# Down projection with seven products per pair of tiles, five pairs at a time

## The chip, the core and the metric

The kernel runs on one core of a Trainium2 chip. The core has a matrix engine (TensorE, PE; it writes only to the PSUM banks), a vector engine (VectorE, DVE), a scalar engine (ScalarE, ACT), a general engine (GpSimd, POOL) and a queue that starts transfers (SyncE, SP). Each works through its own list of instructions in order, and they meet through semaphores. The metric is the time of one execution on the device in microseconds (us), the median of three runs.

## What is computed

One step of a decoder layer on 536 rows: 16 meta tokens and 512 prompt tokens, and 8 single-token samples; the last part of the layer works on 520 of them (8 + 512), all in fp32. After attention, pooling and the output projection, the part that matters here is

```python
a = jax.nn.silu(jnp.einsum('btd,df->btf', h1, w_gate)) * jnp.einsum('btd,df->btf', h1, w_up)
ff = jnp.einsum('btf,fd->btd', a, w_down)
return layer_norm(DEEPNORM_ALPHA * h1 + ff, ln2_g, ln2_b)
```

with a model width of 2048 (16 tiles of 128) and an inner width of 5632 (44 tiles of 128). The outputs are the new rows and the new caches.

## The kernel before

**Number format.** Every matmul operand is split into a high part, rounded to the PE's one-pass format (fp32r), and the rest: `split` (L177) makes `wh` on ACT (L182) and `wl` on DVE (L183) for a piece of weights, in a ring of five buffers of 512 columns each (`WB`). A product is then three matmuls, high x high, high x low and low x high (`products`, L186, matmuls on L189, L190, L192). Activations lie with the token on the free axis, 520 columns, in two halves of 260 (`HALF`).

**Gate and up.** The 44 inner tiles are taken as 22 pairs, tile i with tile i + 22. For each pair, gate and up (`Set.run`, L962) each compute a 2 x 2 block (two inner tiles by two token halves) with seven products instead of eight, a Winograd form of Strassen's method: sums of the weight quarters are made on DVE (L926), sums of the activations were made once, and the products are accumulated in PSUM and added on DVE and ACT (L972 to L996). A product is 8 x 3 = 24 matmuls, a pair 2 x 7 x 24 = 336. `gate_out` applies SiLU, `up_out` multiplies (L1013, L1014, L1016) and stores the two tiles of `a` to memory (`a_d`, L1015 and L1017). Each pair takes six buffers (two of gate, two of up, one of each `run`) from a ring of 16 rows of 520 columns (`row_tile`).

**Down.** The 44 tiles of `a` are read back in four chunks of 11 (`load_a`, L1050), split, and kept. For every chunk and each of the 16 output tiles `down` (L1061) loads the weights (512 and 192 KB), splits them and runs 11 x 2 x 3 = 66 matmuls; DVE adds the two PSUM halves to `acc[m]` (L1080, L1082). The last chunk runs twice through the output tiles, once for each part of the tokens (264 and 256 columns, `DHALF`), so that its weights are loaded and split twice.

**The end.** After every fourth output tile of the last chunk, `Rows.part` turns four tiles back to tokens on rows (PE transposes, L1109), copies them out (L1111) and takes statistics (L1112). After each part of the tokens `Rows.end` applies the closing LayerNorm on DVE (L1119, L1120, 512 columns each) and stores the result. What the first part leaves runs beside the second part's matmuls.

**Order of the work.** A planner orders the instructions of each engine before the run by estimated times; an instruction that stands earlier in the program has priority where several are ready, and weight loads, weight sums and splits are moved ahead by 400 places (`WPRIO`). On the chip the order is fixed: an engine waits at the head of its queue. The operands of gate and up fill all 56 buffers of 520 columns (`slot`, `NG`); the tiles of `a` later take over these buffers. One memory plan (`Region`, `Pool`) hands parts of the on-chip memory from stage to stage.

Of the kernel before, what the change touches and what calls it, by code (L numbers as in the profile page):

```python
# [22 lines left out]
NTOK = NS + SEQ  # L23
HN = NTOK // 2
# [5 lines left out]
F_TILES = 44  # L30
NPAIR = F_TILES // 2
CH = 11
NCH = F_TILES // CH
ALPHA = 2.0 ** 0.25
# [4 lines left out]
NF = 5  # L39
# [8 lines left out]
NG = 56  # L48
NZ = 19
FRW, RRW, MDW = 18960, 24368, 9880  # L50
WIDTH = {"pts": 512}
# [4 lines left out]
SWAP = [i + 8 if i < 8 else i - 8 if i < 16 else i for i in range(32)]  # L56
HALF = [slice(0, HN), slice(HN, NTOK)]

ASLOTS = [[*range(32, 40), *range(14)], [14, 15, *range(24, 32), *range(16, 24), *range(40, 44)],
          [*range(44, 56), *range(32, 40), 0, 1], [*range(2, 24)]]  # L60
DHALF = [slice(0, NS + 256), slice(NS + 256, NTOK)]


# [1 line left out]
def hybrid_step(ctx, tc, xin, w_in, w_o, w_g, w_u, w_d, w_pool, par_d, cst_d, ident_d, ln2gb, kct_d, vc_d, hist_d,  # L65
                ck_d, cv_d, sp_d, yp, ys, nkp, nvp, npp, nks, nvs, nps):
    nc = tc.nc
    PS = bass.MemoryType.PSUM
    sb = ctx.enter_context(tc.tile_pool(name="sb", bufs=1))
    dp = ctx.enter_context(tc.tile_pool(name="dp", bufs=1, space=bass.MemoryType.DRAM))  # L70
# [70 lines left out]

    h_d = dp.tile([KT, P, NTOK], F32, name="h_d")
    h1_d = dp.tile([KT, P, NTOK], F32, name="h1_d")
    a_d = dp.tile([F_TILES, P, NTOK], F32, name="a_d")

    def row_tile(name, w=NTOK):

        return ap_.tile([P, NTOK], F32, tag="row", name=name, bufs=16)[:, :w]
# [22 lines left out]
    def load_raw(src, name):  # L171
        raw = wp.tile([P, 1024], F32, tag="raw", name=f"raw_{name}", bufs=NRAW)[:, :src.shape[-1]]
        with tc.high_priority(prio[0]):
            nc.sync.dma_start(raw, src)
        return raw

    def split(s, name, lo=None):  # L177

        n = s.shape[-1]
        wh, wl = [sp[0].tile([P, 512], F32R, tag=t, bufs=sp[1])[:, :n] for t in ("wh", "wl")]  # L180
        with tc.high_priority(prio[0]):
            nc.scalar.copy(wh, s)  # L182
            (lo or nc.vector).tensor_sub(wl, s, wh.bitcast(F32))  # L183
        return wh, wl

    def products(out, wh, wl, hi, lo, first, last, onto=False):  # L186

        for j, o in enumerate(out):
            nc.tensor.matmul(o, wh, hi[j], start=first, stop=False, skip_group_check=onto)  # L189
            nc.tensor.matmul(o, wh, lo[j], start=False, stop=False, skip_group_check=onto)  # L190
        for j, o in enumerate(out):
            nc.tensor.matmul(o, wl, hi[j], start=False, stop=last, skip_group_check=onto)  # L192
# [48 lines left out]
    with ExitStack() as sa:  # L241
        act, pa, px = Pool(rr), Pool(mid, fr, rr), Pool(mid)
        ps = sa.enter_context(tc.tile_pool(name="psA", bufs=4, space=PS))
# [176 lines left out]
        out = kv_banks(0)  # L420
# [370 lines left out]
    ps = ctx.enter_context(tc.tile_pool(name="psB", bufs=8, space=PS))  # L791

    def bank(name, w=HN):
        return ps.tile([P, 512], F32, tag="bank", name=name, bufs=8)[:, :w]
# [214 lines left out]
    def up_out(s, go, i):  # L1009
        uo = [row_tile(f"uo{i}_{j}") for j in range(2)]  # L1010
        (c11, c12), (c21, c22) = [[g[:, x] for x in HALF] for g in uo]
        c = s.run(c11, c12, c21, c22)
        nc.vector.tensor_mul(go[0][:, HALF[0]], go[0][:, HALF[0]], c11)  # L1013
        nc.vector.tensor_mul(go[1], go[1], uo[1])  # L1014
        nc.sync.dma_start(a_d[2 * i + 1], go[1])  # L1015
        nc.vector.tensor_mul(go[0][:, HALF[1]], go[0][:, HALF[1]], c)  # L1016
        nc.sync.dma_start(a_d[2 * i], go[0])  # L1017

    g0 = ln1(0, out_proj(0))
    zs1 = out_proj(1, g0)  # L1020
# [24 lines left out]
        up_out(sets[2 * i + 1], gate_out(sets[2 * i], i), i)  # L1045


    acc = []

    def load_a(c):  # L1050
        hi, lo = [], []
        for f in range(CH):
            t = pb.tile([P, NTOK], F32, tag="fill", name=f"af{c}_{f}", bufs=NF)
            nc.sync.dma_start(t, a_d[c * CH + f])
            hi.append(slot(f"ah{c}_{f}", (NTOK,), ASLOTS[c][2 * f]))
            lo.append(slot(f"al{c}_{f}", (NTOK,), ASLOTS[c][2 * f + 1]))
            nc.scalar.copy(hi[f], t)
            nc.vector.tensor_sub(lo[f], t, hi[f].bitcast(F32))
        return hi, lo

    def down(c, m, a, halves, tag=""):  # L1061
        nm = f"d{c}_{m}{tag}"
        out = [bank(f"{nm}_{j}", s.stop - s.start) for j, s in enumerate(halves)]
        for r, (f0, f1) in enumerate(((0, 8), (8, CH))):
            raw = load_raw(w_d[c, m, :, f0 * P:f1 * P], f"{nm}_{r}")
            for g0 in range(f0, f1, 4):
                ge = min(g0 + 4, f1)
                wh, wl = split(raw[:, (g0 - f0) * P:(ge - f0) * P], f"{nm}_{g0}")
                for f in range(g0, ge):
                    sl = slice((f - g0) * P, (f - g0 + 1) * P)  # L1070
                    products(out, wh[:, sl], wl[:, sl], [a[0][f][:, s] for s in halves], [a[1][f][:, s] for s in halves],
                             f == 0, f == CH - 1)
        if c == 0:
            acc.append(row_tile(f"acc{m}"))
            hb = pb.tile([P, 2, HN], F32, tag="fill", name=f"h1b{m}", bufs=NF).rearrange("p a b -> p (a b)")
            nc.sync.dma_start(hb, h1_d[m])
        for o, s in zip(out, halves):
            t = acc[m][:, s]
            if c == 0:
                nc.vector.scalar_tensor_tensor(t, hb[:, s], ALPHA, o, op0=ALU.mult, op1=ALU.add)  # L1080
            else:
                nc.vector.tensor_add(t, t, o)  # L1082

    a_cur = load_a(0)
    for c in range(NCH - 1):
        for m in range(KT):
            down(c, m, a_cur, HALF)
            if m == 0:
                a_nxt = load_a(c + 1)
        a_cur = a_nxt  # L1090


    pb.close()
    pb, zp = Pool(fr), Pool(Region("mid_c", F32, MDW))
    gb = [[pb.tile([P, 512], F32, name=f"gb{i}_{q}") for q in range(4)] for i in range(2)]
    for i in range(2):
        for q in range(4):
            nc.sync.dma_start(gb[i][q], ln2gb[i:i + 1, q * 512:(q + 1) * 512].to_broadcast([P, 512]))

    class Rows:  # L1100
        def __init__(self, c0, n, dst):
# [22 lines left out]
    for h, rr in ((0, rows[:3]), (1, rows[3:])):  # L1124
        for m in range(KT):
            down(NCH - 1, m, a_cur, [DHALF[h]], f"h{h}")
            if m % 4 == 3:
                for x in rr:
                    x.part(m // 4)
        for x in rr:  # L1130
            x.end()


# [88 lines left out]
```

## Time and profile before

| what | value |
|---|---|
| median of 3 runs | 1990.83 us (1987.53 to 1991.93) |
| the profiled execution: its time, its span | 1997.12 us, 1995.3 us |
| granted PE clock, mean | 0.992 |
| gate and up, seven-product part | about 617 to 1460 us |
| down projection, chunks 0 to 2 | about 1460 to 1840 us |
| last chunk and closing LayerNorm | about 1840 to 1995 us |
| moved by transfers | 277.57 MB |

The profile is of one execution. A line gives engine, source line, operation and tile names, `out<-in`, and durations; "idle before" is the time the engine waited ahead of it, and the name behind the arrow is what ended that wait. A window's row gives the busy time of the five engines in a stretch, then the granted clock, the busy share of the 16 transfer engines and GB/s. Durations of DVE instructions overlap a little where none of them waits: the next starts before the one before has been confirmed.

### The profile page before, as it was taken

How to read it: one execution, taken by the hardware profiler on the slowest of the kernel's cores; microseconds unless marked ns; L12 is line 12 of the kernel's file. 1: busy time of each engine (PE TensorE's matmuls, PEld its weight loads, DVE VectorE, ACT ScalarE, POOL GpSimd, SP SyncE). 2: the span in 40 equal slices, each digit the busy share in tenths (PEclk: the TensorE clock that was granted, in tenths of full speed). 3: DMA queues.
4: the chain of work that ended last, by engine and by line, in shares of the span. 5: the costliest groups of instructions: out<-in, count | busy, mean ns of one | idle time of the engine just before them, and what ended most of it. 6: DMA issues, size and time to landing. Idle time of an engine off the chain costs nothing.

```text
span 1995.3 us, 39815 instructions
## 1 busy us (share of the span) xinstructions
PE 1960.8 (98%) x16051; PEld 1932.7 (97%) x16051; DVE 1336.8 (67%) x2450; ACT 898.1 (45%) x1749; POOL 2.5 (0%) x8
## 2 busy tenths in 40 slices
PE   8999999999999999999999999999999999999996
PEld 8999999999988999999999999999999999999996
DVE  6666657666777888787777777787763533433586
ACT  6644445544654444445554555445542322222442
POOL 0000000000000000000000000000000000000000
PEclk9999999999999999999999999999999999999998
DMA  8732222665754444333333333333374633323554
GB/s 262 226 102 69 65 79 85 198 202 169 243 162 146 143 149 154 127 121 119 118 108 128 113 130 97 129 115 128 114 249 129 197 106 98 113 88 102 165 177 137
DMA packets 106201, 277.57 MB, mean 139 GB/s; under 512 B 12240, under 2 KB 35352, under 8 KB 105912
## 3 DMA queue, kind: packets, MB, share of 16 engines
q1 hardware_dynamic: 104896, 272.93, 42.5%
q8 instruction: 126, 2.06, 0.4%
q10 hardware_dynamic: 1120, 2.10, 0.4%
q14 instruction: 59, 0.48, 0.1%
HBM read 250.11 MB, written 27.41 MB: 139 GB/s over the span
## 4 chain that ended last, share of the span: by engine, by line
PE 94%; DVE 2%; DMA 2%; ACT 1%; issue 0%; SPq 0%; DVEq 0%; ACTq 0%
PE p_u L189 7%; PE p_u L192 7%; PE p_u L190 7%; PE p_g L192 7%; PE p_g L189 7%; PE p_g L190 7%; PE d L192 6%; PE d L190 6%; PE d L189 6%; PE o L189 3%; PE o L192 3%; PE o L190 3%; PE mm_q L189 2%; PE mm_u L189 2%; PE mm_u L192 2%; PE mm_u L190 2%
## 5 line engine op out<-in xcount | busy, mean ns | idle before, releaser
L182 ACT CAST rr<-fr 128x512 fp32r<-128x512 f32 (+1 forms) x1056 | 639.5, 612 | 918.6 <-PE d L190 248.6
L183 DVE TENSOR_TENSOR rr<-fr,rr 128x512 fp32r<-128x512 f32 (+1 forms) x1056 | 698.2, 677 | 411.3 <-ACT rr L182 399.1
L926 DVE TENSOR_TENSOR fr<-fr 128x1024 f32<-128x1024 f32 x176 | 215.3, 1224 | 71.2 <-DMA fr<-in_w_g_dram 39.0
L192 PE MATMUL p_g<-rr 128*128 128x260 f32 x800 | 226.5, 283 | 2.4 <-DVE rr L183 2.4
L189 PE MATMUL p_u<-rr 128*128 128x260 f32 x800 | 226.8, 284 | 1.3 <-DVE fr L991 1.3
L189 PE MATMUL p_g<-rr 128*128 128x260 f32 x800 | 227.2, 284 | 0.5 <-DVE fr L991 0.5
L192 PE MATMUL p_u<-rr 128*128 128x260 f32 x800 | 225.5, 282 | 0.0
L190 PE MATMUL p_g<-rr 128*128 128x260 f32 x768 | 217.3, 283 | 0.0
L190 PE MATMUL p_u<-rr 128*128 128x260 f32 x768 | 216.9, 282 | 0.0
L189 PE MATMUL d<-rr 128*128 128x260 f32 x736 | 191.4, 281 | 0.0
L190 PE MATMUL d<-rr 128*128 128x260 f32 x672 | 175.5, 283 | 0.0
L192 PEld LDWEIGHTS p_g<-rr 128*128 128x128 f32 x800 | 151.6, 189 | 2.7 <-DVE rr L183 2.7
L189 PEld LDWEIGHTS p_u<-rr 128*128 128x128 f32 x800 | 150.6, 188 | 1.8 <-DVE fr L991 1.8
L189 PEld LDWEIGHTS p_g<-rr 128*128 128x128 f32 x800 | 151.1, 189 | 0.8 <-DVE fr L991 0.7
L192 PEld LDWEIGHTS p_u<-rr 128*128 128x128 f32 x800 | 151.1, 189 | 0.0
L192 PE MATMUL d<-rr 128*128 128x260 f32 x736 | 148.2, 282 | 0.0
L189 PE MATMUL o<-rr 128*128 128x260 f32 x512 | 146.7, 287 | 0.3 <-ACT rr L182 0.3
L190 PEld LDWEIGHTS p_g<-rr 128*128 128x128 f32 x768 | 144.9, 189 | 0.0
L192 PE MATMUL o<-rr 128*128 128x260 f32 x512 | 144.4, 284 | 0.2 <-DVE rr L183 0.2
L190 PE MATMUL o<-rr 128*128 128x260 f32 x512 | 144.6, 283 | 0.0
L190 PEld LDWEIGHTS p_u<-rr 128*128 128x128 f32 x768 | 144.5, 188 | 0.0
L189 PEld LDWEIGHTS d<-rr 128*128 128x128 f32 x736 | 138.5, 188 | 0.0
(396 smaller groups left out, 4591.2 us busy)
## 6 DMA issues: line engine op xcount, KB each, us to landing
fr<-in_w_g_dram SPq DMA_DIRECT2D x95, 512.0 KB, 4.0
fr<-in_w_u_dram SPq DMA_DIRECT2D x95, 512.0 KB, 4.3
fr<-in_w_d_dram SPq DMA_DIRECT2D x80, 512.0 KB, 3.5
fr<-in_w_o_dram SPq DMA_DIRECT2D x64, 512.0 KB, 4.0
fr<-in_w_in_dram SPq DMA_DIRECT2D x46, 512.0 KB, 4.0
fr<-in_w_d_dram SPq DMA_DIRECT2D x80, 192.0 KB, 2.4
a_d<-fr SPq DMA_DIRECT2D x44, 260.0 KB, 2.5
fr<-a_d SPq DMA_DIRECT2D x44, 260.0 KB, 3.8
```

The source lines that it names most:

```text
L182: nc.scalar.copy(wh, s)
L183: (lo or nc.vector).tensor_sub(wl, s, wh.bitcast(F32))
L189: nc.tensor.matmul(o, wh, hi[j], start=first, stop=False, skip_group_check=onto)
L190: nc.tensor.matmul(o, wh, lo[j], start=False, stop=False, skip_group_check=onto)
L192: nc.tensor.matmul(o, wl, hi[j], start=False, stop=last, skip_group_check=onto)
L926: op(self.q(*t), self.q(*a), self.q(*b))
```

## The change

The down projection takes the seven-product form too, for 20 of the 22 pairs. Inner tiles are the summed dimension here: a pair of inner tiles (2i, 2i + 1) times a pair of output tiles (j, j + 8) times the two token halves is again a 2 x 2 x 2 block. Five pairs (`KP`) are summed in PSUM before DVE adds them out: four chunks of five pairs (`WINO`), each for eight column pairs. Pairs 5 and 16 (`PLAIN`) stay as they were.

- **In gate and up**, `up_out` no longer stores the two tiles of `a` for these 20 pairs. It forms four sums `t1` to `t4` on DVE (260 columns each), splits the first quarter (260 columns) and three two-part rows (520 columns each) into high and low, and stores seven operands to `t_d` in seven transfers. It takes nine more rows of the ring of 16. The two plain pairs store `a` as before.
- **Into the down projection**, the PSUM banks are regrouped: two sets of three banks (`tri`) in place of eight single ones. The memory of rows, raw weights and splits is handed over: eight accumulators of 4 x 260 columns, five raw weight buffers of 1280 columns, four split buffers of 640. `load_ops` brings seven operands of five pairs, 35 buffers of the 56; the first of them follow the last up set's operands in the ring. The accumulators start as ALPHA x h1, loaded and scaled on ACT.
- **`column_pair`** is a generator. It loads two raw tiles, and runs the products 1, 7, 2, 6, 4, 5, 3, each with one split of 640 columns and 15 matmuls; four of them need a weight sum of 640 columns first. DVE adds PSUM into the accumulator four times (520, 260, 520 and 520 columns); a product that adds on to the same bank follows after one other product, and product 3 comes after product 1 of the next column pair. The operands of the next chunk are loaded after columns 0 to 3 and 7.
- **At the end** the four plain inner tiles run over 16 output tiles for each part of the tokens: 4 x 3 matmuls for each, with a split of 512 columns and one addition on DVE. Their weights come in four transfers per four output tiles, in runs of 512 bytes, into one, later two buffers. The LayerNorm around them is the same; the loads of `gb` move behind output tiles 1 and 2.

```diff
@@ up_out
-        nc.sync.dma_start(a_d[2 * i + 1], go[1])
         nc.vector.tensor_mul(go[0][:, HALF[1]], go[0][:, HALF[1]], c)
-        nc.sync.dma_start(a_d[2 * i], go[0])
+        if i in PLAIN:
+            for j in range(2):
+                nc.sync.dma_start(a_d[2 * [*PLAIN].index(i) + j], go[j])
+            return
+        (b11, b12), (b21, b22) = [[g[:, x] for x in HALF] for g in go]
+        t12, t34 = row_tile(f"t12_{i}"), row_tile(f"t34_{i}")
+        (t1, t2), (t3, t4) = [[g[:, x] for x in HALF] for g in (t12, t34)]
+        nc.vector.tensor_sub(t1, b12, b11)
+        nc.vector.tensor_sub(t2, b22, t1)
+        nc.vector.tensor_sub(t3, b22, b12)
+        nc.vector.tensor_sub(t4, b21, t2)
+        r = row_tile(f"sb_{i}")
+        hi, lo = [r[:, x] for x in HALF]
+        nc.scalar.copy(hi.bitcast(F32R), b11)
+        nc.vector.tensor_sub(lo.bitcast(F32R), b11, hi)
+        nc.sync.dma_start(t_d[i, 0].rearrange("p a c -> p (a c)"), r)
+        for n, x in ((1, go[1]), (3, t12), (5, t34)):
+            hi, lo = row_tile(f"sh{n}_{i}"), row_tile(f"sl{n}_{i}")
+            nc.scalar.copy(hi.bitcast(F32R), x)
+            nc.vector.tensor_sub(lo.bitcast(F32R), x, hi)
+            for j, y in enumerate((hi, lo)):
+                nc.sync.dma_start(t_d[i, n:n + 2, :, j, :].rearrange("n p c -> p n c"),
+                                  y.rearrange("p (n c) -> p n c", n=2))
@@ down projection: load_a and the chunks' down() go, and in their place:
+    def load_ops(c, n):
+        ts = [slot(f"op{c}_{n}_{i}") for i in WINO[c]]
+        for t, i in zip(ts, WINO[c]):
+            nc.sync.dma_start(t.bitcast(F32), t_d[i, {1: 0, 2: 1, 3: 2, 5: 3, 6: 4, 7: 5, 4: 6}[n]])
+        return ts
...
+        prod(1, al, A[0, 0])
+        yield
+        prod(7, ga, add((1, 0), (0, 0), (1, 0), nc.vector.tensor_sub))
+        nc.vector.tensor_add(ac[:, 1:3, :], ac[:, 1:3, :], tri[:, 0::2, :])
+        prod(2, de, A[0, 1])
+        prod(6, al, add((1, 0), (1, 1), (1, 0), nc.vector.tensor_sub), False)
+        nc.vector.tensor_add(ac[:, 0, :], ac[:, 0, :], al)
+        prod(4, ga, A[1, 1], False)
+        prod(5, al, add((0, 0), (1, 0), (0, 0), nc.vector.tensor_add), False)
+        nc.vector.tensor_add(ac[:, 0:2, :], ac[:, 0:2, :], tri[:, 0::2, :])
+        s4 = add((0, 1), (0, 1), (1, 0), nc.vector.tensor_sub)
+        yield
+        prod(3, al, s4, False)
+        nc.vector.tensor_add(ac[:, 2:4, :], ac[:, 2:4, :], tri[:, 1:3, :])
+        yield
...
+        for j in range(8):
+            g = column_pair(c, j, ops[c])
+            next(g)
+            if before:
+                next(before)
+            next(g)
+            before = g
+            if c + 1 < NCH:
+                for n in ORDER[j:j + 1] if j < 4 else ORDER[4:] if j == 7 else ():
+                    ops[c + 1][n] = load_ops(c + 1, n)
...
+    def down(h, m):
+        if m % 4 == 0:
+            pw[h] = plp.tile([P, 4, 4, P], F32, tag="pl", name=f"pl{h}_{m}", bufs=len(plp.rings["pl"][0]))
+            for f, (c, x) in enumerate(places):
+                nc.sync.dma_start(pw[h][:, :, f, :], w_d[c, m:m + 4, :, x * P:(x + 1) * P].rearrange("m p c -> p m c"))
+        hs = DHALF[h]
+        out = bank(f"d{h}_{m}", hs.stop - hs.start)
+        wh, wl = split(pw[h][:, m % 4], f"dp{h}_{m}")
+        for f in range(4):
+            products([out], wh[:, f, :], wl[:, f, :], [ah[f][:, hs]], [al_[f][:, hs]], f == 0, f == 3)
+        nc.vector.tensor_add(acc[m][:, hs], acc[m][:, hs], out)
```

More of the change, by code (lines that the diff above doesn't have):

```diff
@@ L1061, in down @@
[L1061 to L1072, printed above, removed]
-        if c == 0:
[L1074 to L1082, printed above, removed]
@@ new lines, in hybrid_step @@
+    low = fr.take(4 * 1280)
+    accp.ring("acc", 2 * NTOK, F32, 8)
+    up = [fr.take(1280) for _ in range(3)]
+    fr.give(low, 4 * 1280)
+    rp.rings["wd"] = [[(fr, x) for x in up + [fr.take(1280) for _ in range(2)]], 1280, 0]
+    plp = Pool(fr)
+    plp.ring("pl", 2048, F32, 1)
+    acc4 = []
+    def load_ops(c, n):
[3 more added lines that the diff above has]
+        return ts
@@ L1093, in hybrid_step @@
+    next(before)
+    acc = [acc4[m % 8][:, 2 - 2 * (m // 8):4 - 2 * (m // 8), :].rearrange("p a c -> p (a c)") for m in range(KT)]
+    scope.close()
+    ps, banks = ctx.enter_context(tc.tile_pool(name="psD", bufs=8, space=PS)), 8
+    rp.close()
     pb.close()
     pb, zp = Pool(fr), Pool(Region("mid_c", F32, MDW))
+    places = [x for i in PLAIN for x in PLAIN[i]]
+    pw = {}
+    def down(h, m):
[9 more added lines that the diff above has]
+        nc.vector.tensor_add(acc[m][:, hs], acc[m][:, hs], out)
@@ L1095, in hybrid_step @@
     gb = [[pb.tile([P, 512], F32, name=f"gb{i}_{q}") for q in range(4)] for i in range(2)]
[L1096 to L1098 removed]
+    plp.rings["pl"][0].append((fr, fr.take(2048)))
+    gb_loads = [(i, q) for i in range(2) for q in range(4)]
     class Rows:
```

97 lines of the change are left out of this document (67 added, 30 removed).

## The prediction, made before the changed kernel was run

> **What bounds the kernel now.** I read the page first, then busy time by stage, then who waited for whom, then the queues of VectorE (DVE) and SyncE (SP) around single events.
>
> ```profile
> span 1995.3 us, 39815 instructions
> PE 1960.8 (98%) x16051; PEld 1932.7 (97%) x16051; DVE 1336.8 (67%) x2450; ACT 898.1 (45%) x1749; POOL 2.5 (0%) x8
> PE 94%; DVE 2%; DMA 2%; ACT 1%; issue 0%; SPq 0%; DVEq 0%; ACTq 0%
> ```
>
> TensorE (PE) is busy 98% of the span and is 94% of the chain that ended last. Stage by stage (columns: PE busy and count, weight loads, DVE, ACT, POOL, granted clock, DMA share, GB/s):
>
> ```profile
> 700.00:1000.00 300.00, 300.00 (x2504) 300.00 (x2503) 242.76 (x363) 145.39 (x260) 0.00 (x0) 1.00 0.40 130
> 1600.00:1800.00 200.00, 200.00 (x1673) 200.00 (x1672) 69.84 (x133) 48.07 (x83) 0.00 (x0) 1.00 0.33 102
> 1910.00:1977.00 67.00, 65.17 (x547) 64.33 (x547) 53.30 (x113) 30.60 (x56) 0.00 (x0) 1.00 0.52 163
> 1977.00:1996.00 19.00, 0.86 (x8) 0.53 (x5) 13.57 (x33) 1.48 (x4) 0.00 (x0) 0.64 0.31 110
> ```
>
> In gate and up (first row) PE never pauses and DVE is busy 81%. In the down projection (second) DVE has 35%. So a matmul removed is time saved, at 200/1673 = 0.1195 us each, as long as DVE and the transfers keep up. The last row is the closing LayerNorm, on DVE.
>
> **The change, part by part.** *Matmuls.* The down projection has 44 inner tiles x 16 output tiles x 2 halves x 3 = 4224. After: 4 column-pair chunks x 8 x 7 products x 5 x 3 = 3360, plus plain 16 x 2 x 4 x 3 = 384. That is 480 fewer: **-57.4 us**. A product takes 15 x 0.1195 = 1.79 us, a column pair 105 matmuls, 12.55 us.
>
> *Operands in gate and up.* Durations (busy and mean ns before the last bar):
>
> ```profile
> L183 DVE TENSOR_TENSOR rr<-fr,rr 128x512 fp32r<-128x512 f32 x976 | 654.7, 687 | 353.2 <-ACT rr L182 341.1 <-DMA fr<-in_w_d_dram 6.3 <-PE mm_u L192 1.2
> L926 DVE TENSOR_TENSOR fr<-fr 128x1024 f32<-128x1024 f32 x176 | 215.3, 1224 | 71.2 <-DMA fr<-in_w_g_dram 39.0 <-DMA fr<-in_w_u_dram 29.0
> L1082 DVE TENSOR_TENSOR fr<-fr,d 128x260 f32<-128x260 f32 x64 | 24.3, 421 | 26.9 <-PE d L192 26.9
> L1058 DVE TENSOR_TENSOR rr<-fr,rr 128x520 fp32r<-128x520 f32 x32 | 21.8, 697 | 9.5 <-ACT rr L1057 9.2
> L1112 DVE BATCH_NORM_STATS2 fr<-mid_c 128x6 f32<-128x512 f32 x16 | 10.3, 671 | 2.1 <-ACT mid_c L1111 2.1
> L1057 ACT CAST rr<-fr 128x520 fp32r<-128x520 f32 x19 | 11.8, 627 | 12.3 <-DMA fr<-a_d 9.0 <-PE d L192 2.9
> ```
>
> Each of 20 pairs adds on DVE five instructions of 260 columns (0.42) and three of 520 (0.70): 4.2 us; on ACT one of 260 and three of 520, about 2.3 us; on SP seven stores in place of two. A pair lasts 336 x 0.1195 = 40.2 us, of which DVE idles 19%, 7.6 us. On average it fits; the question is when. The end of a pair, on DVE:
>
> ```profile
> 1010.95 1.23 DVE L926 TENSOR_TENSOR fr<-fr 128x1024 f32<-128x1024 f32 x1 [3.18 <-DMA fr<-in_w_g_dram]
> 1013.63 0.42 DVE L991 TENSOR_TENSOR fr<-fr,p_u 128x260 f32<-128x260 f32 x1
> 1015.62 0.70 DVE L1014 TENSOR_TENSOR fr<-fr 128x520 f32<-128x520 f32 x1
> 1017.56 1.22 DVE L926 TENSOR_TENSOR fr<-fr 128x1024 f32<-128x1024 f32 x1
> 1018.70 0.42 DVE L1016 TENSOR_TENSOR fr<-fr,p_u 128x260 f32<-128x260 f32 x1
> 1020.17 2.49 DVE L183 TENSOR_TENSOR rr<-fr,rr 128x512 fp32r<-128x512 f32 x4
> 1025.00 0.69 DVE L183 TENSOR_TENSOR rr<-fr,rr 128x512 fp32r<-128x512 f32 x1 [0.48 <-ACT rr L182]
> ```
>
> DVE is held 3.18 us by a weight transfer and then runs from 1010.95 to about 1024.5 without a pause. PE resumes about 1014.1, one product of 24 matmuls takes 2.87 us, so up's last product ends near 1017.0 and the third of the next set (product 6) starts near 1022.7; its splits come at 1020.17: a lead of about 2 us. The new work begins exactly there, behind L1016. PE already loses a little at this spot (chain of waits, waits, and the 300 us around it):
>
> ```profile
> 1014.11 0.39 PE p_u L189
> PE p_u L189 <- DVE fr L991: 1.3, 2, 0.8
> 1000.00:1300.00 300.00, 299.18 (x2494) 298.98 (x2493) 230.44 (x334) 148.41 (x272) 0.00 (x0) 1.00 0.37 119
> ```
>
> The change adds a wait too. A pair now takes 15 of the 16 row buffers, so the next gate's `p_g` lies where this pair's `go1` was, and ACT's copy of product 1 (L972) waits for `t4`; behind it on ACT stand the weight casts, and PE's product 6 waits for that copy. The deadline is some 5 us after up's end, `t4` is four short instructions behind L1016; it is near. (The first six pairs' product 1 is mostly made ahead, so not for them.) On SP:
>
> ```profile
> 1013.74 0.33 SPq L174 DMA_DIRECT2D fr<-in_w_u_dram  x1
> 1019.15 0.33 SPq L1017 DMA_DIRECT2D a_d<-fr  x1
> 1023.99 4.71 SPq L174 DMA_DIRECT2D fr<-in_w_u_dram  x3
> ```
>
> The stores fall into the gap before the next weight loads; one that waits past 1024 delays them. Bounds: 0 (all in DVE's idle time) to 2.2 us a pair (4.2 of work less the lead of 2), 44 us. I take 0.6 a pair, nearer the idle time, because weight splits have priority 400 and go first where both are ready: **+12 us**.
>
> *The new products.* Steps between DVE instructions without a wait are shorter than durations: (2.49 - 0.69)/3 = 0.60 for 512 columns, 1018.70 - 1017.56 = 1.14 for 1024, so 0.735 for 640. A column pair needs 7 splits and 4 weight sums of 640, three accumulations of about 0.61 and one of 0.34: 10.3 us of 12.55, or 82%; by durations (0.82, 0.70, 0.42) 11.5, or 92%. ACT needs 7 casts of about 0.75 (0.63 for 520), 5.2 us. Four places make PE wait for DVE to read a PSUM bank; each is covered by one product (1.79), against one instruction in progress (0.74), the read (0.70) and the hand-over. Bounds: 0, since gate and up at 81% lose next to nothing, to 0.9 a column pair (two of four reads late by half an instruction, 0.4 to 0.5), 29 us. I take 0.15 x 32: **+5 us**, nearer the row at 81%.
>
> *Into the down projection.* 35 operand tiles of 260 KB, 9.3 MB, go into buffers that the last up set's operands hold; the first are free after its product 1, 17.2 us before its end (T).
>
> ```profile
> 1465.00:1470.00 5.00, 5.00 (x45) 5.00 (x44) 3.26 (x6) 2.83 (x5) 0.00 (x0) 1.00 1.02 364
> fr<-a_d SPq DMA_DIRECT2D x44, 260.0 KB, 3.8
> ```
>
> At 364 GB/s they take 25.6 us, to T+8.4 if the queue never idles, and seven stores (1.9 MB, 5.1 us) come between; the first column pair wants its fifth operand at T+7.2, its last at T+12.6. Also, `acc` 0 lies in rows that `t34` and `sb` of the last pair hold until about T+5; then the load (3.8), ACT's scaling (0.63) and the first add (0.61) end at T+10, and product 6 wanted that bank at T+5.4. These overlap: I take 6.5 us of stall. What a stall does to the clock:
>
> ```profile
> 614.00:616.00 2.00, 0.91 (x8) 0.70 (x6) 0.61 (x1) 0.00 (x0) 0.00 (x0) 1.00 0.68 234
> 616.00:618.00 2.00, 0.73 (x3) 0.73 (x4) 2.00 (x4) 0.62 (x1) 0.00 (x0) 0.76 0.10 41
> 618.00:620.00 2.00, 2.00 (x11) 2.00 (x10) 0.58 (x2) 0.00 (x0) 0.00 (x0) 0.50 0.78 244
> 620.00:622.00 2.00, 2.00 (x17) 2.00 (x16) 0.27 (x1) 0.50 (x1) 0.00 (x0) 0.89 0.05 18
> 626.00:628.00 2.00, 2.00 (x19) 2.00 (x18) 2.00 (x3) 1.62 (x4) 0.00 (x0) 1.00 0.06 20
> ```
>
> After 2.4 us without matmuls the clock was 0.50, and 10 matmuls (8 + 2 against 19) were lost: 1.2 us more. Together **+8 us**, bounds 3 and 15.
>
> A stall of 2 us in gate and up would lie between that one and the 0.8 us after which the clock stayed at 1.00; I price it without a loss of clock. With 1.2 us for each of 20 pairs, rival (b) below would be 24 us dearer. The Trainium skill (TensorE: Matmul & The Clock Gate, Part 1: The HAM clock gate) says that the clock halves after an idle window of about 3.4 us, so by it those 24 us would never be paid. This trace dropped after 2.4 already, and the trace decides: part of (b) stays above my range.
>
> *Between chunks* operand buffers come free a column pair ahead: 0. *Plain weights* come in runs of 512 bytes, unknown here; nearest are loads and stores in runs of 1040:
>
> ```profile
> 450.00:560.00 110.00, 109.37 (x844) 106.12 (x843) 74.93 (x132) 60.01 (x104) 0.00 (x0) 1.00 0.59 192
> ```
>
> 192/0.59 = 325 GB/s when full; at that rate the 6.3 MB of the first half (weights and `gb`) take 19 of its 28 us, at half of it 39. Bounds 0 and 11, I take **+2 us**.
>
> *The end.* The second half's PE work shrinks from 67 us to 192 x 0.1195 + 32 transposes x 0.109 = 26.4, but the first half's LayerNorm stands in the same DVE queue:
>
> ```profile
> 1932.21 2.72 DVE L1120 SCALAR_TENSOR_TENSOR mid_c<-mid_c,fr 8x512 f32<-8x512 f32 x4
> 1986.22 5.38 DVE L1120 SCALAR_TENSOR_TENSOR mid_c<-mid_c,fr 128x512 f32<-128x512 f32 x8
> 1907.71 0.98 PE tz L1109 x9
> ```
>
> A step is (5.38 - 0.74)/7 = 0.66, also for 8 rows. DVE needs 24 x 0.66 + 16 x (0.60 + 0.34) + 8 x 0.62 + about 1 = 37 us, of which four splits (2.4) are made before. The cover that hid LayerNorm is gone: **+9 us**, bounds 4 and 13. The tail of 18 us stays.
>
> **Sum:** -57.4 + 12 + 5 + 8 + 2 + 9 = -21.4 us. The profiled execution took 1997.1, 1.8 around its span, 6 above the median; from it 1975.7, so from the median **1969 us**.
>
> **Rivals.** (a) *All hidden but the seams*: DVE's 7.6 us of idle a pair and 82% afterwards speak for it; the 13 us without pause against. -57.4 + 3 + 6 = -48: 1943. (b) *Slower: DVE's order in gate and up.* The operands stand ahead of the splits, PE loses 2.0 us in each of 20 pairs: -57.4 + 40 + 24 = +7: 1998. It decides from (57.4 - 24)/20 = 1.7 us a pair. For it: the lead of 2 us, DVE in strict order, `p_g`'s new wait; against: that the same point lost 0.8 at most. (c) *The new products are DVE's*: 0.6 us late a column pair, 19: 1983; the 92% speak for it, the splits made ahead in four buffers against.
>
> **How the numbers follow.** Forecast 0.48, (a) 0.20, (b) 0.18, (c) 0.14. Low end 1943 from (a), raised a little since its seams may cost more: 1945. High end: (b), with another 4: 2002. The forecast's own range is 1955 to 1980. What three rounds can tell from no change is 0.2%, 4 us. Faster: all of the forecast and (a), half of (c): 0.74; same, the rest of (c) and the edge of (b): 0.09; slower 0.17.
>
> **What would show it.** 480 fewer matmuls; 40.2 us a pair in gate and up still (right: waits of PE on splits or on L972's copy below 15 us in all); a gap of PE at the start of the products behind operand loads or the first `acc` add; DVE near 82% in the products with column pairs of 12.7; DVE without a pause after the first plain half. It is wrong if PE's waits in gate and up pass 30 us, if the products take over 13 us a column pair, or if the end has no DVE backlog.

## The result, and the profile after

The changed kernel takes 2092.27 us, the kernel before 1991.38 beside it: ratio 1.0511, 95% interval 1.0493 to 1.0529. Forecast were 1969 us and a range up to 2002; it is 101 us slower than before. Two executions further below are not counted, one of the kernel before (3474 us) and one of the last version (2821 us), which ran at granted clocks of 0.76 and 0.61. Line numbers of the changed kernel are those of before plus 3 or 4 up to the operand making; after it, L1096 loads operands, L1106 weights, L1116 h1, L1117 scales h1, L1128 makes a weight sum, L1135, L1138, L1141 and L1145 add to an accumulator after products 7, 6, 5 and 3. L185 casts and L186 subtracts in a split.

The page's head, its chain of waits, and busy time by stage (columns as in the prediction):

```profile
span 2091.4 us, 39425 instructions
PE 1948.1 (93%) x15571; PEld 1899.7 (91%) x15571; DVE 1546.5 (74%) x2746; ACT 961.1 (46%) x1821; POOL 2.5 (0%) x8
...
PE 64%; DVE 14%; DMA 14%; issue 4%; ACT 2%; SPq 0%; DVEq 0%; ACTq 0%
```

```profile
700.00:850.00 150.00, 150.00 (x1250) 149.94 (x1249) 135.34 (x219) 76.12 (x134) 0.00 (x0) 1.00 0.52 168
850.00:1150.00 300.00, 288.91 (x2361) 284.55 (x2360) 239.95 (x373) 152.27 (x287) 0.00 (x0) 1.00 0.45 144
1489.00:1556.00 67.00, 41.75 (x290) 40.52 (x291) 32.74 (x49) 23.93 (x36) 0.00 (x0) 0.82 0.81 290
1600.00:1800.00 200.00, 177.23 (x1365) 172.84 (x1366) 137.28 (x196) 66.02 (x92) 0.00 (x0) 0.96 0.51 180
```

The 480 matmuls are gone (15571 against 16051), and yet PE's share of the chain fell from 94% to 64%. Three places lost time. In gate and up PE is full from 700 to 850 us, although VectorE (DVE) is busy 90% there, and loses from 850 on, where DVE has 80%: a first sign that load isn't the cause. At the seam (1489 to 1556) 290 matmuls ran where 560 fit. In the new products 1365 ran in 200 us in place of 1673. What PE waited for, over the whole span (us in all, times, longest):

```profile
PE tri L195 <- DVE rr L186: 42.5, 24, 2.8
PE tri L192 <- DVE fr L1135: 30.2, 8, 17.0
PE p_g L192 <- ACT rr L185: 8.6, 15, 0.6
PE p_g L195 <- DVE rr L186: 8.4, 15, 0.8
PE tz L1212 <- DVE fr L1197: 8.2, 4, 5.7
PE p_g L192 <- DVE fr L995: 5.7, 11, 1.1
```

The stages can be bounded by the first and last matmul into each kind of bank. First the kernel before, then the changed one (count, ns least, median and most, first and last start):

```profile
L189 PE MATMUL p_g<-rr x800: 277/283/472, 606.9 to 1439.7; 128*128 128x260 f32 x160
L189 PE MATMUL p_u<-rr x800: 277/283/389, 626.5 to 1460.3; 128*128 128x260 f32 x160
```

```profile
L192 PE MATMUL p_g<-rr x800: 277/283/473, 602.1 to 1468.2; 128*128 128x260 f32 x160
L192 PE MATMUL p_u<-rr x800: 277/283/387, 617.2 to 1488.1; 128*128 128x260 f32 x160
L192 PE MATMUL tri<-rr x664: 277/283/420, 1489.6 to 2011.0; 128*128 128x260 f32 x166
```

Gate and up went from 853.4 to 886.0 us: +32.6. Seam and products took 522.9 us, where 3360 matmuls at 0.1195 are 401.5; about 30 of the plain matmuls (3.6 us) fall into this stretch too, here and in the versions below.

What a column pair waits for stands in DVE's own order of instructions (start, duration, line, shape; in brackets the idle time ahead and what ended it):

```profile
1691.73 0.42 DVE L1138 TENSOR_TENSOR fr<-fr,tri 128x260 f32<-128x260 f32 x1
1692.20 0.82 DVE L186 TENSOR_TENSOR rr<-fr,rr 128x640 fp32r<-128x640 f32 x1
1697.55 0.82 DVE L1128 TENSOR_TENSOR fr<-fr 128x640 f32<-128x640 f32 x1 [4.52 <-DMA fr<-in_w_d_dram]
1698.29 0.82 DVE L186 TENSOR_TENSOR rr<-fr,rr 128x640 fp32r<-128x640 f32 x1
1699.02 0.69 DVE L1141 TENSOR_TENSOR fr<-fr,tri 128x520 f32<-128x520 f32 x1
...
1707.19 0.82 DVE L186 TENSOR_TENSOR rr<-fr,rr 128x640 fp32r<-128x640 f32 x1
1713.10 0.83 DVE L1128 TENSOR_TENSOR fr<-fr 128x640 f32<-128x640 f32 x1 [5.08 <-DMA fr<-in_w_d_dram]
```

The split at 1692.20 is that of product 3 of column pair j. It is the last reader of a weight buffer, and only then can the load that takes that buffer be issued. With five buffers this is the second half of column pair j+2. The very next instruction in DVE's queue is the first weight sum of j+2, which needs that load. So DVE stands for 4.5 to 5.1 us, the whole time of a 640 KB load, and the split at 1698.29, for a product that PE wants now, stands behind it. It recurs every 15.0 to 15.6 us, one column pair; 12.55 were forecast.

### The profile page after: what moved, and what is told of

It is laid out like the page before. It is cut to its first block, busy times and chain, and to the rows that moved or that the text cites. A ratio compares the mean times of both kernels' runs of the same rounds, so it can differ in the third digit from the quotient of the medians.

```text
span 2091.4 us, 39425 instructions
## 1 busy us (share of the span) xinstructions
PE 1948.1 (93%) x15571; PEld 1899.7 (91%) x15571; DVE 1546.5 (74%) x2746; ACT 961.1 (46%) x1821; POOL 2.5 (0%) x8
## 4 chain that ended last, share of the span: by engine, by line
PE 64%; DVE 14%; DMA 14%; issue 4%; ACT 2%; SPq 0%; DVEq 0%; ACTq 0%
DVE rr L186 7%; DMA fr<-in_w_d_dram 6%; PE p_u L195 5%; PE p_u L192 5%; PE p_u L193 5%; PE p_g L192 4%; PE p_g L195 4%; PE p_g L193 4%; PE tri L195 3%; PE tri L192 3%; PE tri L193 3%; DMA fr<-in_w_u_dram 3%; PE o L192 3%; PE o L195 3%; PE o L193 3%
## 5 line engine op out<-in xcount | busy, mean ns | idle before, releaser
L185 ACT CAST rr<-fr 128x512 fp32r<-128x512 f32 (+1 forms) x1072 | 675.1, 643 | 897.8 <-PE tri L193 241.2
L186 DVE TENSOR_TENSOR rr<-fr,rr 128x512 fp32r<-128x512 f32 (+1 forms) x1072 | 745.0, 713 | 246.8 <-ACT rr L185 239.0
L195 PE MATMUL tri<-rr 128*128 128x260 f32 x664 | 194.7, 293 | 24.1 <-DVE rr L186 22.8
L192 PE MATMUL tri<-rr 128*128 128x260 f32 x664 | 194.2, 292 | 12.6 <-DVE fr L1135 6.6
L193 PE MATMUL tri<-rr 128*128 128x260 f32 x664 | 191.9, 289 | 0.0
L1128 DVE TENSOR_TENSOR fr<-fr 128x640 f32<-128x640 f32 x128 | 104.7, 819 | 107.2 <-DMA fr<-in_w_d_dram 105.3
L192 PEld LDWEIGHTS p_g<-rr 128*128 128x128 f32 x800 | 150.4, 188 | 20.4 <-ACT rr L185 11.7
L195 PEld LDWEIGHTS tri<-rr 128*128 128x128 f32 x664 | 129.9, 196 | 29.4 <-DVE rr L186 29.4
L192 PE MATMUL tri<-mid_b,rr 128*128 128x260 f32 x456 | 134.5, 295 | 23.8 <-DVE fr L1135 23.7
L195 PE MATMUL tri<-mid_b,rr 128*128 128x260 f32 x456 | 134.8, 296 | 20.1 <-DVE rr L186 19.7
L195 PEld LDWEIGHTS p_g<-rr 128*128 128x128 f32 x800 | 151.1, 189 | 0.4 <-DVE rr L186 0.4
L192 PE MATMUL o<-rr 128*128 128x260 f32 x512 | 146.0, 286 | 0.3 <-ACT rr L185 0.3
```

Of the source, the lines that this page charges most:

```text
L1128: op(A[t], A[a], A[b])
```

## The experiments

Each starts from the changed kernel unless it says otherwise. The diffs are shortened, and some names in them stand for longer expressions. A line `issue_after(x)` or `after(x)` puts an instruction behind x in its engine's queue, with no other wait.

**Products: the order of the weight sum.**

```diff
         prod(1, al, A[0, 0])
+        with tc.issue_after(last_split):
+            s7 = add((1, 0), (0, 0), (1, 0), nc.vector.tensor_sub)
         yield
-        prod(7, ga, add((1, 0), (0, 0), (1, 0), nc.vector.tensor_sub))
+        prod(7, ga, s7)
```

> Edit: in the new products the first weight sum of a column pair is held behind the split of that column pair's product 1 in VectorE's queue; nothing else is changed. Theory 'order': in the changed kernel this sum stands a column pair too early, straight behind the split that gives its weight buffer free, so VectorE waits 4.4 to 5.0 us for a load in nearly every column pair and the next product's split stands behind it. Then VectorE's 105 us of waits for w_d loads go below 25 us, a column pair falls from 15.4 to 12.6 to 13.0 us, and the time falls by 65 to 85 us, to 2007 to 2027 us. Rival 'load': the 11 us of VectorE work in a column pair of 12.55 us are what makes TensorE wait; the order is no matter; the column pair stays at 15.1 to 15.5 us and the time at 2080 to 2100 us. Rival 'supply': five weight buffers are too few, the load comes as late for the sum at its new place; the wait stays above 70 us and the time above 2060 us.

Measured: 2033.96 us, 58.3 less; ratio to the kernel before 1.0210 (1.0192 to 1.0228). Between 1600 and 1800 us DVE no longer waits for w_d at all. Load and supply both fall as causes of the large part: the same instructions and the same five buffers are there. But the column pair stays at 13.4 us, not 12.6 to 13.0, and the gain misses its lower end by 7. DVE's timeline shows what is left:

```profile
1703.11 0.83 DVE L186 TENSOR_TENSOR rr<-fr,rr 128x640 fp32r<-128x640 f32 x1 [2.77 <-ACT rr L185]
1703.96 0.82 DVE L1128 TENSOR_TENSOR fr<-fr 128x640 f32<-128x640 f32 x1
...
1716.54 0.82 DVE L186 TENSOR_TENSOR rr<-fr,rr 128x640 fp32r<-128x640 f32 x1 [2.80 <-ACT rr L185]
```

DVE is idle 2.8 us in each column pair, waiting for a cast, and the cast waits for PE to leave one of the four split buffers. The buffers go round in the order in which the products are written. PE's queue had them in another order: product 1 of the next pair ahead of 4 and 5 of this one. So the split of 7 waits for the buffer of 4, which PE leaves one product before it wants 7.

**Gate and up: other rows for product 1's copy.**

```diff
-            r = row_tile(f"p_{self.name}")
+            r = row_tile(...) if filled_or_first else pb.tile([P, 2, HN], F32, tag="fill", bufs=NF, ...)
```

> Edit: where a set's product 1 isn't filled ahead, its copy goes into one of the five tiles of the early fills, which lie idle by then, in place of the next of the 16 row buffers; all else as in the changed kernel. Theory 'row ring': the 32 us lost in gate and up begin where product 1's copy comes into use (850 us on) because its row is that of the pair's go1, which the new operand work holds; with other rows PE's waits in gate and up fall from 26 us to below 10 and the time by 15 to 25 us, to 2067 to 2077 us. Rival 'queue load': the new instructions themselves, on ScalarE (hi copies that stand waiting ahead of weight casts) and VectorE, cost the time; the waits stay above 20 us and the time within 6 us of 2092.

Measured: 2060.20 us, 32.1 less, more than the 15 to 25 expected. The stretch from 850 to 1150 us is full again, with the same operand work on DVE and ScalarE (ACT):

```profile
850.00:1150.00 300.00, 299.92 (x2499) 299.64 (x2499) 254.98 (x398) 160.06 (x305) 0.00 (x0) 1.00 0.46 154
```

2499 matmuls against 2361, at DVE 85% busy. So the five subtractions of 260 columns, the three of 520 and the casts cost PE nothing; the ring of 16 rows cost it 32 us. The two rows that meet there, in the changed kernel (`t4` of the last pair reads its row `go1`, then product 1's copy takes that row's place in the ring):

```profile
1068.83 0.42 DVE L1032 TENSOR_TENSOR fr<-fr 128x260 f32<-128x260 f32 x1
1069.82 0.37 ACT L976 COPY fr<-p_g 128x260 f32<-128x260 f32 x1
```

**Gate and up alone.** The kernel before, with the operand making added behind L1014 to L1017 of before and the old down projection:

```diff
         nc.sync.dma_start(a_d[2 * i], go[0])
+        if i in (5, 16): return
+        # t1 to t4, their high and low parts and seven stores, as in the change
```

> Edit: the kernel before with only the operand making of the change added in gate and up (its stores beside the two that were there); the down projection is the old one and the operands aren't used. It measures this part by itself, nine stores a pair in place of seven. If the three losses of the changed kernel (gate and up, transition, products) are separate and additive, gate and up costs 30 to 36 us here too: 2021 to 2028 us. If the loss in gate and up was made by the other parts (the new buffers' places, loads that start earlier), it is below 15 us: under 2006 us. The blind prediction had 12 us for it: 2003 us.

Measured: 2026.43 us against 1991.06 (ratio 1.018, 1.0165 to 1.0195): +35.4, with nine stores a pair in place of seven. The loss belongs to this part; nothing of the new down projection is needed for it.

**How the late copy costs PE its time: two tries without a gain.** In these gates PE's queue takes product 2 ahead of 6, because 6 waits for the copy, and the casts are planned as 5 (first half), 4 (second), 3 (first), 5 (second). The first try holds casts and subtractions in the written order:

```diff
+            with tc.issue_after(last_cast):
                 nc.scalar.copy(wh, s)
```

> Edit, from the changed kernel: in gate and up the weight casts on ScalarE and the splits' subtractions on VectorE are held in the order in which the products are written (1, 7, 6, 2, 5, 4, 3); product 1's copy keeps its place in the ring of rows, behind the last pair's t4. In the changed kernel the second half of product 4 and the first of product 3 are cast ahead of the second half of product 5, in every gate after a pair that makes operands, and in e3_p_elsewhere, where the copy has other rows, they aren't. Theory 'order behind the late copy': the three pauses of PE in each such gate (0.6, 0.8 and 0.7 us, 2.1 us a pair) come from that order, which the writer of the queues chose because the copy is late; with the casts in order most of the 32 us goes: 2062 to 2075 us. Theory 'the late copy itself': product 6 or 5 waits for the copy and the bank whatever the order of the casts; the loss stays above 24 us: 2084 to 2096 us.

Measured: 2100.43 us, 8.2 more (6.1 more against the kernel before beside it), above both expected ranges. The unusual order was not the cause. The second try writes the products in the order in which PE takes them:

```diff
-            prod 7, 6, 2, 5, 4, 3
+            prod 7, 2, 4, 6, 5, 3      # gates that compute product 1 in their own turn
```

> Edit, from the changed kernel: in a gate set whose product 1 isn't filled ahead (from the second pair on that computes it in its own turn) the products are written 1, 7, 2, 4, 6, 5, 3 in place of 1, 7, 6, 2, 5, 4, 3; product 1's copy keeps its late row. In the changed kernel TensorE takes 2 ahead of 6 in these gates, since 6 waits for the copy, while the five split buffers go round in the written order, so the split of 5 waits for a buffer that 6 holds and that is read late. e5_casts_in_order, with the casts held in the written order, made it worse (2100 us), so the order of the casts was not the cause. Theory 'split buffers out of order': with the written order the one that TensorE takes, the copy may be late without harm: PE's pauses of 2.1 us a pair fall below 0.8, 2062 to 2075 us. Theory 'the late copy itself': product 6 waits as long, or the later part of the gate is pressed together: 2084 us or more.

Measured: 2102.76 us, 10.5 more (9.9 against the kernel before beside it). The waits of PE, from 850 to 1488 us, left the gate and came back in the up set behind it:

```profile
PE p_u L192 <- ACT rr L185: 19.1, 30, 0.6
PE p_u L195 <- DVE rr L186: 4.7, 8, 1.3
```

So neither order made up for the late row; other rows did. By which path the copy's delay becomes three pauses of some 0.5 to 0.8 us in each pair isn't settled: that the split buffers get out of step, as in the products, fits the waits, but the run meant to show it gained nothing. With the copy elsewhere all other rows come free earlier as well (14 or 13 of 16 are taken in a pair); that can't be told from the copy's own row either.

**The seam: the order of the loads.** PE's longest wait, 17.0 us, ends with DVE's first add to accumulator 0, which waits for ACT's scaling of h1, which waits for the load. In the changed kernel:

```profile
1512.05 1.40 ACT L1117 ACTIVATE fr<-fr 128x520 f32<-128x520 f32 x2 [1.60 <-DMA fr<-h_d]
1513.47 0.69 DVE L1135 TENSOR_TENSOR fr<-fr,tri 128x520 f32<-128x520 f32 x1 [14.76 <-ACT fr L1117]
```

```diff
+        ts = [slot(..., at=FREED[q + x])]          # operands into the buffers that come free first
+            t = accp.tile(..., at=(6, 4, 5, 7, 0, 1, 2, 3)[j])
+                with tc.issue_after(last_operand_load):   # for accumulators 1 to 7
                     nc.sync.dma_start(h, h1_d[...])
```

> Edit: the operand tiles of the first chunk take the buffers in the order in which the last up set leaves them, accumulator 0 lies where rows come free first of the eight, and h1 of accumulators 1 to 7 is loaded behind the last operand load. Theory 'order of the loads': the 32 us lost between up's last product and the products' steady part come from h1 of accumulator 0, loaded nearly last among 9.3 MB of operands and other h1, with VectorE's add (14.8 us of wait) and PE behind it. Then the loss falls to 8 to 14 us and the time by 18 to 24 us, to 2068 to 2075 us. Rival 'volume': 9.3 MB of operands, 4.3 MB of h1 and the first weights need over 40 us at the 290 to 360 GB/s of that stretch whatever their order; the loss stays above 25 us and the time above 2085 us.

Measured: 2083.35 us, only 8.9 less, between the ranges of both theories (its executions lie between 2079.91 and 2094.94). SyncE's (SP) queue shows what had been left out of the account. After the first chunk's operands and h1 come 17 operands of the next chunk, four plain weight loads and gb, all ahead of the weights of the third column pair, for which DVE then stands 4.4 us more:

```profile
1507.49 3.04 SPq L1101 DMA_DIRECT2D mid_b<-t_d  x4
1510.58 9.34 SPq L1101 DMA_DIRECT2D rr<-t_d  x13
1520.28 2.79 SPq L1196 DMA_DIRECT2D fr<-in_w_d_dram  x4
1523.12 1.78 SPq L1237 DMA_DIRECT2D fr<-in_ln2gb_dram  x1
...
1526.43 0.38 SPq L1111 DMA_DIRECT2D fr<-in_w_d_dram  x1
```

```profile
1533.00 0.83 DVE L1134 TENSOR_TENSOR fr<-fr 128x640 f32<-128x640 f32 x1 [4.42 <-DMA fr<-in_w_d_dram]
```

The loads were issued as early as a buffer was free, not as late as they could be.

**All three put right, in two steps.** First the products written in PE's order (with the held sum), and the copy's other rows:

```diff
+    # written order: 7(j), 3(j-1), 2(j), 6(j), 1(j+1), 4(j), 5(j)
```

> Edit, from the changed kernel: product 1's copy in the idle tiles of the early fills (as in e3_p_elsewhere), and the new products written in the order in which TensorE takes them, 7(j), 3(j-1), 2(j), 6(j), 1(j+1), 4(j), 5(j), so that the four split buffers go round in that order too; the first weight sum of a column pair is held behind the split before it. In e1_sum_order a column pair still took 13.4 us: its split of product 7 waited for the buffer of product 4, which TensorE had moved behind product 1 of the next pair and ended only 1.8 us before it wanted product 7. Theory 'buffers out of order': the remaining 0.5 us of PE behind the add after product 7, with VectorE's 2.8 us of idle time before it, goes; a column pair takes 12.6 to 12.8 us, 18 to 25 us less than in e1_sum_order; with the 32 us of e3_p_elsewhere the time is 2034 - 32 - 22 = 1980, 1975 to 1986 us. Rival 'VectorE is full': 10.6 us of work in 12.55 us can't be placed without PE waiting; the column pair stays at 13.3 us or more and the time at 1998 to 2006 us.

Measured: 1974.61 us; ratio 0.9915 (0.9899 to 0.9932), 0.9% below the kernel before. So the rival 'VectorE is full' falls. Then the loads:

```diff
+                with after(weights_of_this_pair, j):
                     nc.sync.dma_start(h, h1_d[...])
+                with after(casts_of_last_pair, j):
                     nc.scalar.activation(h, h, AF.Copy, scale=ALPHA)
-            for n in ORDER[j:j + 1] if j < 4 else ...        # next chunk's operands
+            for n in ORDER[j - 2:j - 1] if 2 <= j < 6 else ...
+                with after(weights_of_next_pair): load_ops   # also the plain weights and gb
```

> Edit, beside that of c1_products_and_p: operand tiles take the buffers in the order in which the last up set leaves them; accumulator 0 lies in rows that the last pair doesn't use; h1 of a later accumulator is loaded behind that column pair's weights and scaled behind the casts of the column pair before; the next chunk's operands, the plain weights and gb are loaded behind the weights that were being loaded too early before. In e2_transition_order two gaps were left: 7.9 us behind the second half of h1 of accumulator 0, and 8 us (with half clock) behind weights of the third column pair that stood in the queue after 17 operands of the next chunk, four plain loads and gb. Theory 'order of the loads': the transition costs 5 to 12 us in place of 32, the time is 20 to 27 us below that of c1_products_and_p. Rival 'volume' (9.3 MB of operands at 380 GB/s are 24.5 us, of which 17 lie before the seam, and the last pair's stores and first weights add 3 MB): the products wait for operands one after the other, the transition still costs over 18 us, and the gain on c1_products_and_p is below 14 us.

Measured: 1948.83 us; ratio 0.9786 (0.9769 to 0.9803). That is 25.8 us below the step before, within the 20 to 27 expected, and it beats both kernels, by 43 us and by 143. The products in it, one row by stage and one instruction (the add after product 5) in two column pairs that follow each other:

```profile
1650.00:1750.00 100.00, 100.00 (x837) 100.00 (x836) 85.21 (x120) 40.98 (x56) 0.00 (x0) 1.00 0.58 196
```

```profile
1711.45 0.70 DVE L1157 TENSOR_TENSOR fr<-fr,tri 128x520 f32<-128x520 f32 x1 [0.16 <-PE tri L195]
...
1724.02 0.70 DVE L1157 TENSOR_TENSOR fr<-fr,tri 128x520 f32<-128x520 f32 x1 [0.16 <-PE tri L195]
```

PE doesn't pause, DVE is busy 85%, and a column pair takes 12.57 us. The seam:

```profile
1450.00:1480.00 30.00, 26.14 (x209) 25.09 (x208) 25.09 (x39) 13.44 (x20) 0.00 (x0) 1.00 1.00 360
```

3.9 us are lost there, less than the 5 to 12 expected, at 360 GB/s and with the clock at 1.00; in the changed kernel it was 0.82.

Now the last matmul into `tri`, from the last into `p_u`, divides the loss. The rows of three versions: the sum held; the products in PE's order as well, with the copy's other rows; the loads held too.

```profile
L192 PE MATMUL p_u<-rr x800: 277/283/389, 621.2 to 1488.1; 128*128 128x260 f32 x160
L192 PE MATMUL tri<-rr x664: 277/283/506, 1489.3 to 1951.7; 128*128 128x260 f32 x166
```

```profile
L192 PE MATMUL p_u<-rr x800: 277/283/388, 619.4 to 1454.3; 128*128 128x260 f32 x160
L192 PE MATMUL tri<-rr x664: 277/283/390, 1455.6 to 1891.9; 128*128 128x260 f32 x166
```

```profile
L192 PE MATMUL p_u<-rr x800: 277/283/388, 618.8 to 1453.7; 128*128 128x260 f32 x160
L192 PE MATMUL tri<-rr x728: 277/283/390, 1455.0 to 1866.1; 128*128 128x260 f32 x182
```

522.9 us in the changed kernel, 463.6, 437.6 and 412.4: the sum's order 59.3, the split buffers' order 26.0, the loads' order 25.2.

**The end.** The prediction's +9 us was the LayerNorm of the first half in DVE's queue. First it was moved away:

```diff
+                if h == 0:
+                    nc.scalar.activation(z, z, AF.Identity, scale=r, bias=nb)
+                    nc.gpsimd.tensor_mul(z, z, gb[0][q][:n]); nc.gpsimd.tensor_add(z, z, gb[1][q][:n])
```

> Edit, beside c2_and_load_order: the first half's closing LayerNorm leaves VectorE: ScalarE applies mean and deviation in one activation, GpSimd multiplies by the gain and adds the bias (24 operations of 0.66 us less on VectorE, 12 more on ScalarE, 24 on GpSimd). Theory 'backlog', the one of the blind prediction's +9 us for the end: PE loses 8.0 us to the accumulator adds that stand behind those operations in VectorE's queue; without them PE ends 6 to 8 us sooner and the time falls by 5 to 8 us, to 1941 to 1944 us. Rival 'the tail moves': what comes last is the second half's own statistics and norm, or GpSimd takes longer for its 24 operations than VectorE's 15.8 us and holds the buffers or slows VectorE; then the time stays within 3 us of 1949 or rises.

Measured: 1961.33 us (ratio 0.9848, 0.9834 to 0.9862), 12.3 more than the same kernel without it, which was run beside it:

> The same kernel as c2_and_load_order, beside c3_first_norm_off_DVE on one chip: 1946 to 1952 us, ratio to the kernel before 0.977 to 0.981.

Measured: 1949.07 us, ratio 0.9786 (0.9772 to 0.9800), as the first time. What slowed the other is one instruction of DVE, for which PE waited 16.5 us, while GpSimd (POOL) ran its multiplications and additions one behind the other:

```profile
1916.35 16.76 DVE L186 TENSOR_TENSOR rr<-fr,rr 128x512 fp32r<-128x512 f32 x1
```

```profile
1910.82 2.50 POOL L1249 TENSOR_TENSOR mid_c<-mid_c,fr 8x512 f32<-8x512 f32 x2 [1907.72 <-PE d L193]
...
1930.08 10.48 POOL L1250 TENSOR_TENSOR mid_c<-mid_c,fr 128x512 f32<-128x512 f32 x8
```

So the run said nothing on the backlog, and the operations were left out instead:

```diff
+                if h:      # second half only
                     nc.vector.scalar_tensor_tensor(z, z, mu, gb[0][q][:n], ...)
                     nc.vector.scalar_tensor_tensor(z, z, r, gb[1][q][:n], ...)
```

> Edit, beside c2_and_load_order: the 24 closing operations of the first half's LayerNorm (16.3 us by 0.68 us each on VectorE) are left out, so the rows of the first half go out without mean, deviation, gain and bias applied; nothing takes their place. Theory 'backlog': VectorE is without a pause from 1894 us to the end of c2_and_load_order and PE's 8.0 us of waits at the transposes come from it; without the 24 operations PE waits below 2 us, and the time falls by 6 to 9 us, to 1940 to 1943 us. It can't fall further, because the second half's PE work and the 17 us of its own norm remain. Rival: what slowed c3_first_norm_off_DVE was the moved order of the other instructions and not GpSimd; then this kernel too has an instruction of VectorE that lasts over 10 us, and gains nothing.

Measured: 1943.99 us (1940.25 to 1944.90), 4.8 less by the medians and 7.6 by the ratios (0.9748, 0.9727 to 0.9770, against 0.9786), where 6 to 9 were expected. No DVE instruction lasts long in it, so the rival of the moved order falls. The stage shows the gain more plainly. Last matmul into `tri` and last transpose, without the norm and then with it:

```profile
L192 PE MATMUL tri<-rr x728: 277/283/390, 1460.2 to 1872.5; 128*128 128x260 f32 x182
L1234 PE MATMUL tz<-fr x80: 270/272/327, 1874.3 to 1924.5; 128*128 128x128 f32 x64, 128*8 128x128 f32 x16
```

```profile
L1234 PE MATMUL tz<-fr x80: 270/272/476, 1868.0 to 1927.2; 128*128 128x128 f32 x64, 128*8 128x128 f32 x16
```

52.0 us against 61.1 from one to the other, and PE's 8.0 us of waits at the transposes are gone: the backlog costs PE 9.1 us. The profiled execution had come 6 us later to that stage, so time and stage can't be told apart to better than some 5 us.

## Why the prediction was wrong, point by point

| term of the sum | predicted (bounds) | measured | from |
|---|---|---|---|
| 480 matmuls | -57.4 | -57.4 | count, and 837 in 100 us in the version put right |
| operands in gate and up | +12 (0 to 44) | +33 to +35 | stage +32.6; alone +35.4; other rows -32.1 |
| new products | +5 (0 to 29) | +85 | 59.3 + 26.0 |
| into the down projection | +8 (3 to 15) | +29 | 25.2 + 3.9 |
| between chunks | 0 | 0 | 1650 to 1750 in the version put right, PE 100.00 |
| plain weights | +2 (0 to 11) | 0 | PE's largest wait at `d` 0.3 |
| end | +9 (4 to 13) | +9 | 9.1 of PE in the version put right |

The measured terms make +99 to +101, the median moved by +101. That they meet so closely is partly luck. Products and seam can be divided only to some 3 us (the stretch 1489 to 1556 of the changed kernel lost 32 by itself, 67 less 290 x 0.1195), and the spans of the two profiled executions differ by 96.

*The new products* are the step that failed. It went by amounts: 10.3 us of DVE work in 12.55, and what late reads of PSUM cost at 82%. The amounts were right; 12.57 us a column pair at 85% show it, and with the queues in order the term is about 0. What the step never did is follow one buffer round: when its last reader runs, when its load can start, where the first reader stands. For the five weight buffers that is a load of 4.5 to 5.1 us straight in DVE's path; for the four split buffers a lead of one product in place of three. Both had their signs in the text: weight sums are moved ahead by 400 places, and the generators interleave product 1 of the next pair. The bound of 29 us came from the same reasoning and so held neither. Rival (c) named the right engine and the wrong cause.

*Gate and up* had its mechanism in the text, `p_g`'s wait on `t4`, with the six pairs that escape it; the trace shows just that onset at 850 us. The failed step is the size, "I take 0.6 a pair, nearer the idle time, because weight splits have priority 400": 2.1 us a pair, 15 pairs. DVE's 13 us without a pause, the other ground for a loss there, was none. 2.1 us a pair is above the 1.7 from which rival (b) decides, but that price was for 20 pairs: 15 make 32 us, at the edge of the 33.4 that (b) needs. (b) named `p_g`'s new wait too, but put the loss on the operands that stand ahead of the splits, and these cost nothing. The waits named in the changed kernel's profile, 23 us for gate and up, stay under the mark of 30 that was set, though the stage lost 33. The rest is counted as busy: from 850 to 1150 us a matmul has 288.91/2361 = 0.122 us of busy time, with the copy elsewhere 299.92/2499 = 0.120.

*The seam*: the wait for accumulator 0's h1 was named and put at T+10; it ended at 1513.5, T+25. The step that failed counted what the products need (operands, stores, accumulator 0) and not what else SP would be given early: other accumulators' h1, the next chunk's operands, plain weights, gb. At 290 GB/s each megabyte of these is 3.4 us.

*The end* was right, as far as the version put right can show it, and the sign set for the products, column pairs over 13 us, showed at once. The price of clock that the prediction weighed for gate and up didn't arise there: the pauses are 1.1 us at most and the granted clock stays at 1.00. In the changed kernel's products it did arise, though not each time: behind a pause of 2.42 us that ended at 1750.29 the clock was 0.50 (1752 to 1754 us), behind one of 2.45 us that ended at 1684.17 it stayed at 1.00. At the seam, with a wait of 17 us, it was 0.82 on average.

Rival (a), all hidden but the seams, 1943 us, describes what the change could do: 1948.83 with its queues put right.

## What to carry to other kernels

A busy share says what an engine could carry, not what its queue will do: for every ring of buffers, write down the last reader, the load that it lets go, the first reader of that load and its place in a strict queue, and compare the order in which buffers are handed out with the order in which PE's queue uses them. When work is made early because it can be, ask what stands behind it; all four losses here (the sum, the split buffers, the row, the loads) were cured by order or place, with no work taken off PE, DVE or ACT (15571, 2746 and 1821 instructions, as in the changed kernel).

## What was not expected of the hardware

DVE's subtraction of 512 columns, 0.69 us elsewhere, took 16.76 us while GpSimd ran tensor operations without a gap, some 13 of them, of 1.26 us each. Under the same operations a DVE instruction with an operand in PSUM kept its 0.42 us:

```profile
1912.53 0.42 DVE L1219 TENSOR_TENSOR fr<-fr,d 128x256 f32<-128x256 f32 x1 [0.42 <-PE d L195]
```
The Trainium skill (SBUF — State Buffer, SBUF: two separate sides) says that the two engines share a port pair, which a GpSimd operation holds as an exclusive lock against a DVE operation with two inputs in SBUF, until the instruction ends. Which instructions suffered agrees; but the wait was that of some 13 instructions and not of one, so DVE did not get its turn between them. It isn't so each time: two later subtractions beside the same row of GpSimd operations took 2.37 us together (from 1937.24 us on). The moved work came to 30 us on GpSimd, and moving it cost 12.
